# One PSUM bank per tile in a pair of half products, and branch weights loaded with a pair's first product

## The chip, the cores and the metric

The kernel runs on one core of one Trainium2 chip. The metric is the device time of one execution in microseconds (us). Times shown are medians of a few executions.

## What is computed

Two layers of a streaming encoder for 640 rows (512 of a prompt and 8 x 16 of decoding requests) of width 1024. Each layer projects its input once, with one wide matrix, splits the columns among four branches (a gated MLP, a recurrence, a latent attention, a memory attention) and their gates, and merges the branches:

```
(a_u, a_v, a_g, b_x, b_g, c_q, c_kv, c_kr, c_g, m_q, gate_logits) = split_cols(x @ w_in)
oa, ob, oc, om = the four branches, three of them times silu of a_g, b_g, c_g
g = sigmoid(gate_logits).reshape(B, T, N_BRANCH, D_MODEL)
ya, yb, yc, ym = oa @ w_br_a, ob @ w_br_b, oc @ w_br_c, om @ w_br_m
merged = g[:, :, 0] * ya + g[:, :, 1] * yb + g[:, :, 2] * yc + g[:, :, 3] * ym
x_new = layer_norm(ALPHA * x + merged @ w_out, ln_g, ln_b)
```

All data is float32. Every matrix operand is split into a high part, rounded to the format that TensorE multiplies, and a low part, the remainder; a product is high x high + high x low + low x high.

## The kernel before

**Pairs.** Most columns of `w_in` are done two chunks of 128 columns at a time, as a pair. A pair's product has two halves of output columns, two halves of the 1024 rows of contraction and two halves of the 640 time steps (`lo_` and `hi_`, 320 each). The kernel forms it by a scheme of seven half products in place of eight: sums of weight halves (`ws`, made by `wsum`) meet sums of input halves (`xt[1]` to `xt[4]`), and the results are added and subtracted on the way out. Each half product is one call of `product`: 12 matmuls of 128x128 weights by 320 columns, in one accumulation. `run_pair` writes the seven in this order: `ba` with input 11, `bb` with 21, `ba` with 2 (added to what is there), `bc` with 3, `ba` with 1, `bc` with 4, `ba` with 22. Between them, ScalarE copies a partial result of `ba` or `bc` to SBUF (`copy_out`, line 375) and VectorE adds or subtracts one (`psum`, line 372). Because `ba` and `bc` go on accumulating after such a copy, the next product into the same bank has to wait for it.

**PSUM.** There are eight banks, all given out: tag `acc` has two tiles of two banks each, tag `s` two tiles of one bank, tags `t` and `o` one bank each. `run_pair` takes one `acc` tile, named `fp`, and uses its two banks as `ba` and `bb`; `bc` is a tile of tag `s`, named `fp_c`. The framework puts a wait on an instruction by tile: an instruction that writes a tile waits for the engines that read that tile.

**Weights.** A pair's two raw chunks `r0`, `r1` and a branch's raw weights share the tag `raw`, three buffers, loaded on the queue of SyncE (SP), which works in order. A load waits until the last reader of its buffer is done. `wcast` (ScalarE, line 379) makes the high part, `wlow` (VectorE, line 384) the low part; high parts have three buffers, low parts two.

**Two kinds of pairs.** Each layer has six pairs without a branch (`gelu_pair`, `silu_pair`), whose results are stored, and 14 pairs in `merge_pairs`, whose results are gates: each of these is followed by two branch products `y` (`Branch.run`, `merge_y`, line 121), of 24 matmuls each for branches 0 to 2 and 12 for branch 3. VectorE multiplies a gate by its `y` (line 1112) and adds it to the sum `macc` (line 1116). The two `y` products also take tiles of tag `acc`, so a pair and its branch use three of them in turn.

**What sets the order.** `on` ties products, copies, casts and sums of the pairs on PE, ScalarE (ACT) and VectorE (DVE) to the order in which the code is written; the framework's scheduler places everything else (transposes, the recurrence, layer norms) between them, by its own estimates.

Of the kernel before, what the change touches and what calls it, by code (L numbers as in the profile page):

```python
# [21 lines left out]
TH = T // 2  # L22
# [17 lines left out]
def encoder_step(  # L40
# [30 lines left out]
    def tmp(shape, name="tmp", dtype=F32):  # L71
        return tp.tile(shape, dtype, tag="t", name=name)

    def ftmp(shape, name, dtype=F32):
        return tp.tile(shape, dtype, tag="f", name=name, bufs=2)
# [4 lines left out]
    def acc(name="acc"):  # L80
        return pa.tile([128, 2, 512], F32, tag="acc", name=name)

    def bank_s(name="ps_s"):
        return pb.tile([128, 512], F32, tag="s", name=name, bufs=2)
# [13 lines left out]
    def wtile(tag, n, name, bufs=2):  # L98
        return wp.tile([128, n], F32 if tag in ("raw", "ws") else F32R, tag=tag, name=name, bufs=bufs)

    def wraw(src, n=1024):
        raw = wtile("raw", n, "raw", 3)
        nc.sync.dma_start(out=raw, in_=src)
        return raw
# [95 lines left out]
    for l in range(L):  # L200
# [162 lines left out]
        def on(eng, ins_):  # L363
            order_only(ins_, tail.get(eng))
            tail[eng] = ins_
            return ins_

        def wsum(out, x, y):
            on("DVE", DVE.tensor_tensor(out=out, in0=x, in1=y, op=ALU.add))  # L369

        def psum(out, x, y, op):
            on("DVE", DVE.tensor_tensor(out=out, in0=x, in1=y, op=op))  # L372

        def copy_out(out, in_):
            on("ACT", ACT.copy(out=out, in_=in_))  # L375

        def wcast(src, n):
            h = wtile("wh", n, "wh", 3)
            on("ACT", ACT.copy(out=h, in_=src))  # L379
            return h  # L380

        def wlow(src, h, n):
            lo = wtile("wl", n, "wl")
            on("DVE", DVE.tensor_tensor(out=lo, in0=src, in1=h.bitcast(F32), op=ALU.subtract))  # L384
            return h, lo
# [3 lines left out]
        class Pair:  # L389
# [3 lines left out]
            def load(self):  # L393
                self.r0, self.r1 = (wraw(ins["w_fm"][l, self.c + e]) for e in range(2))
# [22 lines left out]
        def product(o, hl, half, x, first, last):  # L417
            bh, bl = xt[x]
            h, lo = hl
            steps = [(k, h, b) for k in range(4) for b in (bh, bl)] + [(k, lo, bh) for k in range(4)]  # L420
            for n, (k, a, b) in enumerate(steps):
                k0 = half * 512 + k * 128
                on("PE", PE.matmul(  # L423
                    out=o, lhsT=a[:, k0:k0 + 128], rhs=b[:, k, :],
                    start=(first and n == 0), stop=(n == len(steps) - 1), skip_group_check=True,
                ))
# [9 lines left out]
        def run_pair(p, nxt, act, y=None):  # L436

            r0, r1 = p.r0, p.r1
            ab, bc = acc("fp"), bank_s("fp_c")[:, 0:TH]
            ba, bb = (ab[:, j, 0:TH] for j in range(2))  # L440
            z0, z1, t_ = ftmp([128, T], "z0"), ftmp([128, T], "z1"), tmp([128, T], "tu")
            p1, u = t_[:, lo_], t_[:, hi_]
            product(ba, p.w0, 0, 11, True, False)
            copy_out(p1, ba)
            p.low1()
            h2 = wcast(r1, 1024)
            product(bb, p.w0, 1, 21, True, True)
            psum(z0[:, lo_], p1, bb, ALU.add)
            act(0, lo_, z0, z0[:, lo_])
            w2 = wlow(r1, h2, 1024)  # L450
            wsum(r0[:, b_], r0[:, b_], p.ws[:, a_])
            product(ba, p.w1, 0, 2, False, False)
            copy_out(u, ba)
            h3 = wcast(r0[:, b_], 512)
            product(bc, p.w1, 1, 3, True, False)
            copy_out(z1[:, hi_], bc)
            w3 = wlow(r0[:, b_], h3, 512)
            if nxt:
                nxt.load()
            if y:  # L460
                y.cast()
            elif nxt:
                nxt.cast0()
                nxt.sums(0)
            product(ba, w2, 0, 1, False, False)
            psum(z1[:, hi_], z1[:, hi_], ba, ALU.subtract)
            if not y and nxt:
                nxt.sums(1)
            product(bc, w2, 1, 4, False, True)
            psum(z1[:, lo_], bc, u, ALU.subtract)  # L470
            if y:
                y.low()
            if nxt:
                if y:
                    nxt.cast0()
                else:
                    nxt.low0()
            act(1, slice(0, T), z1, z1)
            if not y and nxt:
                nxt.cast1()  # L480
            product(ba, w3, 0, 22, False, True)
            act(0, hi_, z0, ba)
            if y:
                if nxt:
                    nxt.low0()
                    nxt.sums(0)
                    nxt.sums(1)
                    nxt.cast1()
                y.run((z0, z1))

        def gelu_pair(p, nxt):
            def act(e, cols, z, v_):
                on("ACT", ACT.activation(out=ub[:, p.c - FM_U + e, cols], in_=v_, func=AF.Gelu_apprx_tanh))

            run_pair(p, nxt, act)

        def silu_pair(p, nxt, i, c):
            th = [tmp([128, T], f"th{e}") for e in range(2)]
            rest = []

            def act(e, cols, z, v_):
                on("ACT", ACT.activation(out=th[e][:, cols], in_=v_, func=AF.Tanh, scale=0.5))
                rest.append((e, cols, v_))

            run_pair(p, nxt, act)
            for e, cols, v_ in sorted(rest, key=lambda r: -r[0]):
                on("DVE", DVE.scalar_tensor_tensor(
                    out=th[e][:, cols], in0=th[e][:, cols], scalar=1.0, in1=v_, op0=ALU.add, op1=ALU.mult
                ))
            for e in range(2):  # L510
                nc.gpsimd.dma_start(out=gscr[i][c + e], in_=th[e])
# [621 lines left out]
        class Branch:  # L1133
# [2 lines left out]
                self.br = (0, 2, 1, 3)[bi]  # L1136
                self.src = ins["w_brm"][l] if bi == 3 else ins["w_br"][l, self.br]

            def cast(self):
                self.raw = wtile("raw", 2 * self.n, "raw", 3)  # L1140
                nc.sync.dma_start(
                    out=self.raw.rearrange("p (e c) -> p e c", e=2),
                    in_=self.src[self.f:self.f + 2].rearrange("e p c -> p e c"),
                )
                self.h = wcast(self.raw, 2 * self.n)

            def low(self):
# [17 lines left out]
        def merge_pairs(bhl):  # L1165
            bhls[0] = bhl
            ys = [Branch(0, f) for f in (4, 6)] + [Branch(bi, f) for bi in (1, 2, 3) for f in (0, 2, 4, 6)]
            ps = [Pair(22 + y.br * 8 + y.f) for y in ys]
            first_pair(ps[0])
            for n, y in enumerate(ys):  # L1170
                def act(e, cols, z, v_):
                    on("ACT", ACT.activation(out=z[:, cols], in_=v_, func=AF.Tanh, scale=0.5))

                run_pair(ps[n], ps[n + 1] if n + 1 < len(ps) else None, act, y)
                if y.bi == 3 and y.f == 0:
                    merge_split(0)
            for f in (2, 4, 6):
                merge_split(f)
# [221 lines left out]
```

## Time and profile before

| | |
|---|---|
| median of 3 runs | 1487.37 us (1486.15 to 1489.79) |
| the profiled execution, its own time | 1489.98 us |
| span of the profile | 1488.2 us |
| TensorE matmul (PE) busy | 1390.5 us, 93% of the span |
| VectorE (DVE) busy | 985.9 us, 66% |
| ScalarE (ACT) busy | 637.8 us, 43% |
| GpSimd (POOL) busy | 124.3 us, 8% |
| DMA | 183.96 MB, 124 GB/s over the span |

Busy time of PE is from the start of a matmul to its end; matmuls overlap, so the time between two starts is shorter than one lasts. What is left of the span, some 98 us, is time in which no matmul runs at all.

### The profile page before, as it was taken

How to read it: one execution, taken by the hardware profiler on the slowest of the kernel's cores; microseconds unless marked ns; L12 is line 12 of the kernel's file. 1: busy time of each engine (PE TensorE's matmuls, PEld its weight loads, DVE VectorE, ACT ScalarE, POOL GpSimd, SP SyncE). 2: the span in 40 equal slices, each digit the busy share in tenths (PEclk: the TensorE clock that was granted, in tenths of full speed). 3: DMA queues.
4: the chain of work that ended last, by engine and by line, in shares of the span. 5: the costliest groups of instructions: out<-in, count | busy, mean ns of one | idle time of the engine just before them, and what ended most of it. 6: DMA issues, size and time to landing. Idle time of an engine off the chain costs nothing. (4 is left out here: it accounts for less than half of the span.)

```text
span 1488.2 us, 22595 instructions
## 1 busy us (share of the span) xinstructions
PE 1390.5 (93%) x8896; PEld 1257.4 (84%) x8896; DVE 985.9 (66%) x1676; ACT 637.8 (43%) x1159; POOL 124.3 (8%) x254
## 2 busy tenths in 40 slices
PE   8998999999899999999999989999998999899997
PEld 7788887779888988988888988877898889888886
DVE  8767747695656565666885776685855565667656
ACT  6543534455533333444255435444663333334430
POOL 1101100021200000000111012001111000000000
PEclk9999999999999999999999999999999999999999
DMA  7624623244232322236375246132443223222343
GB/s 272 256 79 167 189 77 118 82 172 141 94 98 89 99 71 79 78 93 205 107 229 183 96 152 220 33 118 97 163 143 113 77 78 103 82 76 67 95 146 106
DMA packets 59098, 183.96 MB, mean 124 GB/s; under 512 B 6640, under 2 KB 15760, under 8 KB 55920
## 3 DMA queue, kind: packets, MB, share of 16 engines
q1 hardware_dynamic: 48304, 127.54, 26.9%
q0 software_dynamic: 10688, 54.98, 10.0%
q8 instruction: 70, 1.15, 0.3%
q14 instruction: 36, 0.29, 0.1%
HBM read 148.49 MB, written 32.69 MB: 122 GB/s over the span
## 5 line engine op out<-in xcount | busy, mean ns | idle before, releaser
L384 DVE TENSOR_TENSOR wl<-raw,wh 128x1024 fp32r<-128x1024 f32 (+1 forms) x148 | 153.5, 1049 | 113.6 <-PE fp_c L423 56.7
L379 ACT CAST wh<-raw 128x1024 fp32r<-128x1024 f32 (+1 forms) x148 | 132.3, 910 | 108.8 <-DMA raw<-in_w_br 83.5
L423 PE MATMUL fp<-xh,wh 128*128 128x320 f32 x480 | 147.5, 319 | 24.9 <-ACT tu L375 22.4
L121 PE MATMUL y<-bhl,wh 128*128 128x320 f32 x896 | 145.9, 313 | 12.7 <-ACT wh L379 12.7
L121 PEld LDWEIGHTS y<-bhl,wh 128*128 128x128 f32 x896 | 134.1, 189 | 18.3 <-ACT wh L379 17.9
L423 PE MATMUL fp<-xl,wh 128*128 128x320 f32 x480 | 142.6, 309 | 0.0
L423 PE MATMUL fp<-xt,wh 128*128 128x320 f32 x640 | 110.9, 315 | 27.3 <-DVE z L372 27.3
L423 PEld LDWEIGHTS fp<-xt,wh 128*128 128x128 f32 x640 | 95.5, 188 | 37.4 <-DVE z L372 37.4
L423 PEld LDWEIGHTS fp<-xh,wh 128*128 128x128 f32 x480 | 90.0, 188 | 36.7 <-ACT tu L375 32.5
L121 PE MATMUL fm<-xl,wh 128*128 128x320 f32 x448 | 113.9, 327 | 0.0
L121 PE MATMUL fm<-xh,wh 128*128 128x320 f32 x448 | 112.6, 323 | 0.0
L423 PE MATMUL fp_c<-xt,wh 128*128 128x320 f32 x640 | 106.8, 309 | 0.0
L423 PEld LDWEIGHTS fp_c<-xt,wh 128*128 128x128 f32 x640 | 97.2, 188 | 0.0
L375 ACT COPY tu<-fp 128x320 f32<-128x320 f32 x80 | 34.0, 426 | 139.5 <-PE fp L423 138.5
L423 PEld LDWEIGHTS fp<-xl,wh 128*128 128x128 f32 x480 | 90.2, 188 | 0.1
L423 PE MATMUL fp<-xh,wl 128*128 128x320 f32 x480 | 89.9, 309 | 0.0
L147 DVE TENSOR_TENSOR wl<-raw,wh 128x1024 fp32r<-128x1024 f32 (+3 forms) x67 | 73.9, 1104 | 20.7 <-ACT wh L146 8.3
L146 ACT CAST wh<-raw 128x1024 fp32r<-128x1024 f32 (+3 forms) x67 | 63.9, 953 | 54.8 <-PE fm L121 17.7
L121 PE MATMUL fm<-xh,wl 128*128 128x320 f32 x448 | 86.3, 328 | 0.0
L121 PEld LDWEIGHTS fm<-xl,wh 128*128 128x128 f32 x448 | 75.7, 188 | 8.3 <-issue 6.4
L379 ACT CAST wh<-ws 128x1024 fp32r<-128x1024 f32 x40 | 41.8, 1046 | 91.7 <-DVE ws L369 91.7
L121 PEld LDWEIGHTS fm<-xh,wh 128*128 128x128 f32 x448 | 75.6, 188 | 6.1 <-issue 5.3
(340 smaller groups left out, 2816.5 us busy)
## 6 DMA issues: line engine op xcount, KB each, us to landing
raw<-in_w_fm SPq DMA_DIRECT2D x108, 512.0 KB, 3.7
xsum<-xt POOLq DMA_DIRECT2D x8, 1280.0 KB, 10.6
xt<-xsum POOLq DMA_DIRECT2D x8, 1280.0 KB, 6.1
raw<-in_w_br SPq DMA_DIRECT2D x20, 512.0 KB, 3.6
mcache<-in_mem_kv SPq DMA_DIRECT2D x8, 1024.0 KB, 6.8
raw<-in_w_out SPq DMA_DIRECT2D x16, 512.0 KB, 4.3
osrc<-oscr POOLq DMA_DIRECT2D x20, 320.0 KB, 3.1
gscr<-th POOLq DMA_DIRECT2D x16, 320.0 KB, 2.7
```

The lines of the kernel that those rows point to most:

```text
L121: PE.matmul(out=out[:, j, 0:TH], lhsT=a(k), rhs=b(k)[:, j * TH:(j + 1) * TH], start=(n == 0), stop=(n == len(steps) - 1),)
L146: ACT.copy(out=dst_h, in_=src)
L147: DVE.tensor_tensor(out=dst_l, in0=src, in1=dst_h.bitcast(F32), op=ALU.subtract)
L375: on("ACT", ACT.copy(out=out, in_=in_))
L379: on("ACT", ACT.copy(out=h, in_=src))
L384: on("DVE", DVE.tensor_tensor(out=lo, in0=src, in1=h.bitcast(F32), op=ALU.subtract))
L423: on("PE", PE.matmul(out=o, lhsT=a[:, k0:k0 + 128], rhs=b[:, k, :], start=(first and n == 0), stop=(n == len(steps) - 1), skip_group_check ...
```

## The change

In `run_pair`, `ba` becomes the first bank of an `acc` tile named `fp_a` (its second bank stays unused), and `bb` and `bc` become two tiles of tag `s`, `fp_b` and `fp_c`. In `Branch`, the load of the raw weights moves out of `cast` into a method of its own, `load`, which `run_pair` calls ahead of its first product; `cast` stays where it was, after the load of the next pair's weights.

```
@@ run_pair
             r0, r1 = p.r0, p.r1
-            ab, bc = acc("fp"), bank_s("fp_c")[:, 0:TH]
-            ba, bb = (ab[:, j, 0:TH] for j in range(2))
+            ba = acc("fp_a")[:, 0, 0:TH]
+            bb, bc = (bank_s(f"fp_{n}")[:, 0:TH] for n in "bc")
+            if y:
+                y.load()
             z0, z1, t_ = ftmp([128, T], "z0"), ftmp([128, T], "z1"), tmp([128, T], "tu")
             p1, u = t_[:, lo_], t_[:, hi_]
             product(ba, p.w0, 0, 11, True, False)
@@ class Branch
-            def cast(self):
+            def load(self):
                 self.raw = wtile("raw", 2 * self.n, "raw", 3)
                 nc.sync.dma_start(
                     out=self.raw.rearrange("p (e c) -> p e c", e=2),
                     in_=self.src[self.f:self.f + 2].rearrange("e p c -> p e c"),
                 )
+
+            def cast(self):
                 self.h = wcast(self.raw, 2 * self.n)
```

**TensorE, a pair of the first layer's merge.** The last matmuls of the first half product (into `ba`), the second (into `bb`) and the start of the third (into `ba` again), with the engines whose semaphores a row waits for in brackets. Before:

```order
L423 MATMUL fp<-xh_0_103,wl 128x320 x4
L423 MATMUL fp<-xh_1_104,wh 128x320 [waits Activation_49]
L423 MATMUL fp<-xl_1_106,wh 128x320
...
L423 MATMUL fp<-xh_1_104,wl 128x320 x4
L423 MATMUL fp<-xt_3984,wh 128x320 [waits DVE_49]
L423 MATMUL fp<-xt_3984,wh 128x320 x7
L423 MATMUL fp<-xt_3984,wl 128x320 x4
```

With the change:

```order
L423 MATMUL fp_a<-xh_0_103,wl 128x320 x4
L423 MATMUL fp_b<-xh_1_104,wh 128x320
L423 MATMUL fp_b<-xl_1_106,wh 128x320
...
L423 MATMUL fp_b<-xh_1_104,wl 128x320 x4
L423 MATMUL fp_a<-xt_3990,wh 128x320 [waits Activation_49]
L423 MATMUL fp_a<-xt_3990,wh 128x320 x7
L423 MATMUL fp_a<-xt_3990,wl 128x320 [waits DVE_49]
```

The second product no longer waits for ScalarE; the third waits for ScalarE (the copy of `ba`) where it waited for VectorE (the read of `bb`), and its last four matmuls name VectorE, which makes their low weights. All other pairs show the same.

**SyncE's queue, the start of the first layer's merge** (`in_w_fm` are the pairs' chunks, `in_w_br` a branch's weights, `vec` a small table). Before:

```order
L103 DMA raw<-in_w_fm 128x1024 x4
L519 DMA vec<-in_vecs 128x162
L1141 DMA raw<-in_w_br 128x2x512
L103 DMA raw<-in_w_fm 128x1024 x2
L1141 DMA raw<-in_w_br 128x2x512
```

With the change:

```order
L103 DMA raw<-in_w_fm 128x1024 x2
L1143 DMA raw<-in_w_br 128x2x512
L103 DMA raw<-in_w_fm 128x1024
L521 DMA vec<-in_vecs 128x162
L103 DMA raw<-in_w_fm 128x1024
L1143 DMA raw<-in_w_br 128x2x512
L103 DMA raw<-in_w_fm 128x1024 x2
```

A branch's load stood behind both chunks of the next pair; it now stands ahead of them.

**ScalarE, the first pair of the first layer's merge,** from the copy of the third product (`tu<-fp`) on; `lb` is the recurrence's work. Before:

```order
L1029 ACT_TABLE_LOAD
L1029 ACTIVATE lb_2996<-lb_2996 128x664
L1172 ACT_TABLE_LOAD
L1172 ACTIVATE z_4008<-z_4008 128x320
L375 COPY tu<-fp 128x320
L379 CAST wh<-raw 128x512
L375 COPY z_4009<-fp_c 128x320
L947 ACTIVATE ne<-ne 128x4
L379 CAST wh<-raw 128x1024 x2
```

With the change:

```order
L1176 ACTIVATE z_4017<-z_4017 128x320
L375 COPY tu<-fp_a 128x320
L1031 ACT_TABLE_LOAD
L1031 ACTIVATE lb_3002<-lb_3002 128x664
L379 CAST wh<-raw 128x512
L375 COPY z_4018<-fp_c 128x320
L379 CAST wh<-raw 128x1024 x2
L1176 ACT_TABLE_LOAD
L1176 ACTIVATE z_4018<-z_4018 128x640
```

A table load and the recurrence's square root moved from ahead of the copy of the third product to between it and the copy of the fourth (`z<-fp_c`). Elsewhere the scheduler moved a few transposes, `mix` matmuls and layer-norm steps between the pairs without a branch; the order of the pairs' own work is the same on every engine.

## Rows read from the trace of the kernel before

**Rows 1.** The page's first part: busy time, share of the span, instructions of each engine.

```profile
PE 1390.5 (93%) x8896; PEld 1257.4 (84%) x8896; DVE 985.9 (66%) x1676; ACT 637.8 (43%) x1159; POOL 124.3 (8%) x254
```

**Rows 2.** PE's waits, longest first: total us, times, longest.

```profile
PE fp L423 <- DVE z L372: 29.1, 42, 1.5
PE fp L423 <- ACT tu L375: 22.4, 36, 1.3
PE y L121 <- ACT wh L379: 12.7, 20, 2.3
```

**Rows 3.** PE's groups: busy, mean ns | idle before them, by releaser.

```profile
L423 PE MATMUL fp<-xh,wh 128*128 128x320 f32 x480 | 147.5, 319 | 24.9 <-ACT tu L375 22.4 <-DVE z L372 1.8 <-DVE mixb L660 0.4
...
L423 PE MATMUL fp<-xt,wh 128*128 128x320 f32 x640 | 110.9, 315 | 27.3 <-DVE z L372 27.3
```

**Rows 4.** PE's timeline over one merge pair: start, us, instruction [idle before <-releaser].

```profile
525.51 0.75 PE L423 MATMUL fp<-xh,wl 128*128 128x320 f32 x4
526.77 0.41 PE L423 MATMUL fp<-xh,wh 128*128 128x320 f32 x1 [0.52 <-ACT tu L375]
...
528.04 0.75 PE L423 MATMUL fp<-xh,wl 128*128 128x320 f32 x4
529.45 1.44 PE L423 MATMUL fp<-xt,wh 128*128 128x320 f32 x8 [0.65 <-DVE z L372]
...
531.31 1.34 PE L423 MATMUL fp_c<-xt,wh 128*128 128x320 f32 x8
...
533.07 1.34 PE L423 MATMUL fp<-xt,wh 128*128 128x320 f32 x8
...
537.76 0.75 PE L423 MATMUL fp<-xh,wl 128*128 128x320 f32 x4
539.67 2.61 PE L121 MATMUL y<-bhl,wh 128*128 128x320 f32 x16 [1.15 <-ACT wh L379]
...
549.24 0.41 PE L423 MATMUL fp<-xh,wh 128*128 128x320 f32 x1 [0.52 <-ACT tu L375]
```

**Rows 5.** ACT and DVE in the same pair, timeline of all engines.

```profile
526.29 0.43 ACT L375 COPY tu<-fp 128x320 f32<-128x320 f32 x1 [3.57 <-PE fp L423]
...
528.90 0.49 DVE L372 TENSOR_TENSOR z<-tu,fp 128x320 f32<-128x320 f32 x1 [1.67 <-PE fp L423]
...
538.57 2.00 ACT L379 CAST wh<-raw 128x1024 fp32r<-128x1024 f32 x2 [4.53 <-DMA raw<-in_w_br]
```

**Rows 6.** SyncE's loads in the same pair, timeline of the SP queue.

```profile
530.55 0.33 SPq L103 DMA_DIRECT2D raw<-in_w_fm  x1
534.62 0.38 SPq L1141 DMA_DIRECT2D raw<-in_w_br  x1
```

**Rows 7.** The page's DMA issues: count, size, median us to landing.

```profile
raw<-in_w_fm SPq DMA_DIRECT2D x108, 512.0 KB, 3.7
```

**Rows 8.** A later merge pair, of branch 3: its first product, and its third product's low weights.

```profile
647.40 0.31 PE L423 MATMUL fp<-xh,wh 128*128 128x320 f32 x1
...
650.18 1.22 DVE L384 TENSOR_TENSOR wl<-ws,wh 128x1024 fp32r<-128x1024 f32 x1
```

**Rows 9.** A pair without a branch: the last product waits behind a load.

```profile
142.18 0.33 SPq L103 DMA_DIRECT2D raw<-in_w_fm  x1
...
147.42 0.69 DVE L369 TENSOR_TENSOR ws<-raw 128x512 f32<-128x512 f32 x1 [1.75 <-DMA raw<-in_w_fm]
...
148.75 0.48 DVE L372 TENSOR_TENSOR z<-z,fp 128x320 f32<-128x320 f32 x1
...
149.29 0.41 PE L423 MATMUL fp<-xh,wh 128*128 128x320 f32 x1 [0.91 <-DVE z L372]
```

**Rows 10.** First merge pair of a layer: waits for ACT, in layers 1 and 2.

```profile
393.65 0.42 PE L423 MATMUL fp<-xh,wh 128*128 128x320 f32 x1 [1.32 <-ACT tu L375]
...
1147.20 3.63 PE L121 MATMUL y<-bhl,wh 128*128 128x320 f32 x16 [2.29 <-ACT wh L379]
```

**Rows 11.** A window after that wait: us, busy of each engine, granted clock, DMA share, GB/s.

```profile
1147.00:1152.00 5.00, 4.80 (x22) 4.80 (x23) 3.65 (x4) 2.06 (x4) 1.07 (x2) 0.66 0.66 220
```

More of the change, by code (lines that the diff above doesn't have):

```diff
@@ L438, in run_pair @@
             r0, r1 = p.r0, p.r1
-            ab, bc = acc("fp"), bank_s("fp_c")[:, 0:TH]
-            ba, bb = (ab[:, j, 0:TH] for j in range(2))
+            ba = acc("fp_a")[:, 0, 0:TH]
+            bb, bc = (bank_s(f"fp_{n}")[:, 0:TH] for n in "bc")
+            if y:
+                y.load()
             z0, z1, t_ = ftmp([128, T], "z0"), ftmp([128, T], "z1"), tmp([128, T], "tu")
@@ L1137, in __init__, with load @@
                 self.src = ins["w_brm"][l] if bi == 3 else ins["w_br"][l, self.br]
-            def cast(self):
+            def load(self):
                 self.raw = wtile("raw", 2 * self.n, "raw", 3)
@@ L1144, in cast @@
                 )
+            def cast(self):
                 self.h = wcast(self.raw, 2 * self.n)
```

## The prediction

> **What bounds the kernel now.** The page's first part comes first: PE is busy for 93% of the span, VectorE for 66% and ScalarE for 43% [rows 1]. So the time is PE's own work plus the 97.7 us in which it stands still (1488.2 - 1390.5), and a change that touches no matmul can only give back part of the second. Next I read PE's list of waits. Three of its lines make 64.2 us of the 97.7, and the change touches the code of all three: half products waiting for `z` on VectorE (29.1 us, 42 times), half products waiting for `tu` on ScalarE (22.4 us, 36 times), and branch products waiting for a high part on ScalarE (12.7 us, 20 times) [rows 2].
>
> Which products wait is told by their inputs. Inputs 1 to 4 bear the name `xt`, inputs 11, 21 and 22 the names `xh` and `xl`. PE's groups put 27.3 of the 29.1 us at a product that starts with `xt`, and only 1.8 us at one that starts with `xh` [rows 3]. In the timeline of one pair the picture is plain [rows 4]: the second product starts 0.52 us late, after the copy `tu`; the third starts 0.65 us late, after `z`; the branch product starts 1.15 us late. The second product writes `bb`, and the copy reads `ba`; the third writes `ba`, and `z` reads `bb` [rows 5]. They meet only because both banks are one tile.
>
> **What a wait costs.** A record of idle time is not the whole loss, since matmuls overlap. Two undisturbed products of 12 matmuls start 1.76 us apart (531.31 and 533.07), so a matmul takes 0.147 us of the engine, while its record lasts 0.31 us [rows 4]. A wait that the trace calls 0.52 us therefore also loses 0.31 - 0.147 = 0.163 us of overlap, and the first record after it is 0.10 us longer (0.41 for 0.31, 1.44 for 1.34). I add 0.265 us to each wait. The check: from the second product of this pair (526.77) to that of the next (549.24) are 22.47 us. The pair's seven products and the two of `y` are 84 + 48 = 132 matmuls, 19.36 us; the three waits with their additions are 0.785 + 0.915 + 1.415 = 3.115 us; together 22.48 us. Nothing else is lost in a pair.
>
> **The change, part by part.**
>
> Tiles of their own. The order of the changed kernel has no wait ahead of the second product, and ScalarE's copy in place of VectorE's `z` ahead of the third. The copy has been done since before the second product's start would have been (it ends 0.43 us after it begins at 526.29, and the second product alone lasts 1.76 us [rows 4, 5]), so its wait is covered. Hence all 36 waits for `tu` go: 22.4 + 36 x 0.265 = 31.9 us. Of the waits for `z`, those ahead of `xt` go; three of the 42 lie ahead of `xh` (the last product, after a read of `ba` itself), so 27.3 + 39 x 0.265 = 37.6 us.
>
> What is late next in a merge pair? The third product's low weights, which VectorE makes after the last `y` of the pair before. In the tightest pairs, those of branch 3 (84 + 24 matmuls), they are done at 650.18 + 1.22 = 651.40, which is 4.0 us after the pair's start at 647.40 [rows 8]; without waits PE needs them after 32 matmuls, 4.7 us. A margin of 0.7 us: covered, but not by much.
>
> Loads. A branch's load was issued at 534.62, as the next pair's second chunk was at 530.55, each when a buffer came free, and ScalarE then waited 4.53 us for it [rows 5, 6]. With the change it goes out a pair's length earlier, and its 20 waits go: 12.7 + 20 x 0.265 = 18.0 us. The queue holds as many loads as before; what moves back are the next pair's chunks, to the two times that I just named. The second of them would be issued at about 534.6 and land 3.7 us later (the median of 108 such loads [rows 7]), at 538.3; VectorE adds the chunks only after the low weights of `y` and of the next pair, which follow the last product (it ends near 538.5 [rows 4]) and take over a microsecond. Covered by about 1.5 us. If a load were later than that, the sums would be late, then VectorE's product with `y`, then the `acc` tile that the next pair wants.
>
> The long wait of a layer's first branch product (2.29 us) has a second price: behind it 16 matmuls take 3.63 us where 2.61 us is usual, and the granted clock of the 5 us from 1147 is 0.66, that is, part of it at 1.2 GHz in place of 2.4 [rows 4, 10, 11]. Without the wait 3.63 - 2.61 = 1.0 us more comes back.
>
> What stays. In a pair without a branch the last product (22) waits for a read of `ba` that stands on VectorE behind the sums of the next pair's chunks, and these behind a load, whose buffer comes free in the same pair: issued at 142.18, used at 147.42, then `z` at 148.75 and the product at 149.29, 0.91 us late [rows 9]. If the third product starts 0.92 us earlier, this chain starts only with the second product's end, and the last product may wait that much longer. Five such pairs per layer have a next pair, ten in all: from 0 (the load is early enough) to 10 x 0.915 = 9.2 us. I take 4 us, nearer the lower end, because only three waits of this sort are in the trace. In the first merge pair of each layer, ScalarE and VectorE carry the recurrence (waits of 1.32 us in place of 0.52 [rows 10]), and the new order puts a table load and a square root ahead of the copy that the fourth product of `bc` needs. Two waits of about 1 us may stay there per layer: 4 us, between 0 and the 10 us that stand there now (1.32, up to 1.5 ahead of the third product [rows 2], and 2.29, with additions, twice).
>
> A rule against the change is in the Trainium skill, page Perfetto Trace Analysis, section Matmul Optimizations: all eight PSUM banks should be in use, so that instructions overlap. The change leaves the second bank of `fp_a` idle and uses both one-bank tiles in every pair, with none to spare. By the rows, `bb` was read by 528.90 + 0.49 = 529.39 and is written again at 549.24 [rows 4, 5]; some 20 us lie between, so by them one tile for each is enough, and by the rule the waits would come back as those for a free bank.
>
> **The sum.** 31.9 + 37.6 + 18.0 + 1.0 - 4 - 4 = 80.5 us. The profiled execution took 1489.98 us (span 1488.2 us and 1.8 us around it), so 1409.5 us for such a one; it lies 2.6 us above the median of the runs (1487.37), which gives 1406.9. I predict 1407 us.
>
> **The rivals.**
>
> 1. *The waits are handed on.* PE comes 2 to 3 us earlier per pair, VectorE has the same work, and the third product waits for its low weights, or the last for `z`, in place of `bb`. For it: VectorE is at 66% over all, and the margin in branch 3's pairs is 0.7 us [rows 1, 8]. Against it: in 20 of the 28 merge pairs PE's work is 24 matmuls longer, 3.5 us more room. If the whole of the `z` term stays, 1407 + 37.6 = 1445 us; if it stays in the eight pairs of branch 3 and in all those without a branch, 8 x 0.915 + 9.2 - 4 = 12.5 us, so about 1420 us.
>
> 2. *Only the loads count.* The framework still orders the reads by something that the order does not show, and the products wait as before: 18.0 + 1.0 us come back, 1468 us. Against it is the order itself, which has no wait there.
>
> 3. *Banks run short* (what the Trainium skill's rule on the eight banks would bring). `fp_b` of the next pair would wait for a reader of the one before; at the price of today's wait for `z` in all 40 pairs that is again about 1445 us. The 20 us of room speak against it.
>
> 4. *Slower: the pairs' chunks come late.* The second chunk is now loaded when the branch's weights were, and a late one holds up VectorE's sums, the product with `y` and the next pair's `acc` tile. To eat the 80 us in the 28 merge pairs it would have to hold PE 2.9 us in each. With 1.5 us of cover and some 2 us of VectorE's work that could still slip, this begins at a landing of about 3.7 + 1.5 + 2 + 2.9 = 10 us; above that the kernel is slower. The median is 3.7 us, and ScalarE's wait of 4.53 us for the load issued at 534.62 ended with that load's landing, some 4 us after its issue [rows 5 to 7].
>
> **How the numbers follow.** The forecast, with its own range of 1397 to 1419 us (all 87.5 + 1 us back and a little at the layer's end, or both remainders at their upper ends and 4 us more), has a chance of 0.78. The smaller form of rival 1 (1419 to 1430) has 0.10, its whole form with rival 3 0.07, rival 2 0.02, rival 4 0.02, anything else 0.01. The range of 1396 to 1429 us holds a little over 8 in 10. What a measurement of this kernel can tell from no change is about 0.3%, 4.5 us. Only rival 4, and what I do not see, end within that or above it: faster 0.96, within 0.3% 0.02, slower 0.02.
>
> **What the profile of the changed kernel would show.** PE's waits for `tu` and for `z` ahead of `xt` are gone from its list, or below 3 us each; `y` for ScalarE below 2 us. A merge pair of branches 0 to 2 takes 19.4 us, one of branch 3 15.9 us. PE's busy time falls by the additions alone, 95 x 0.265 = 25 us, to about 1365 us, its idle time from 97.7 to some 43 us, and its share rises to 97%. ScalarE's waits for `in_w_br` are gone. What would prove me wrong: a new line in PE's waits of more than 10 us, for `wl` of line 384 or for a load; or VectorE waiting for `in_w_fm` in the merge.

## The result, and the profile after

The changed kernel takes 1407.31 us (median of four runs, 1406.80 to 1408.88) where the kernel before took 1486.76 us on the same chip (1485.60 to 1489.79). The ratio is 0.9464, with a 95% interval of 0.9448 to 0.9481: 5.4% faster, 79.4 us. 1407 us was predicted.

The first part of the page answers to [rows 1]: busy time, share of the span (now 1405.5 us), instructions.

```profile
PE 1367.4 (97%) x8896; PEld 1257.8 (89%) x8896; DVE 986.3 (70%) x1676; ACT 645.5 (46%) x1159; POOL 122.7 (9%) x254
```

The count of matmuls is the same. PE's busy time is 23.1 us lower and its idle time 38.1 us (1405.5 - 1367.4) in place of 97.7. VectorE and ScalarE do what they did before, in a shorter time.

PE's list of waits, against [rows 2] (total us, times, longest):

```profile
PE fp_a L423 <- DVE z L372: 7.9, 11, 2.4
...
PE y L121 <- ACT z L1176: 0.2, 1, 0.2
```

The line for `tu` is gone. What is left for `y` is a single wait of 0.2 us, and it is for another releaser (ScalarE's read of `fp_a`, line 1176, and not the cast `wh`). For `z`, 7.9 us stand where 29.1 stood. None of them is at an input named `xt`, as PE's groups tell, which answer to [rows 3]; in the timeline all eleven waits stand at product 22:

```profile
L423 PE MATMUL fp_a<-xt,wh 128*128 128x320 f32 x640 | 106.9, 309 | 0.0
L423 PE MATMUL fp_a<-xh,wh 128*128 128x320 f32 x320 | 98.1, 318 | 8.4 <-DVE z L372 7.9 <-DVE mixb L662 0.4
```

The timeline of one merge pair, all engines, answers to [rows 4 to 6] (start, us, instruction, idle before it):

```profile
522.28 0.31 PE L423 MATMUL fp_a<-xh,wh 128*128 128x320 f32 x1
523.22 1.22 DVE L384 TENSOR_TENSOR wl<-ws,wh 128x1024 fp32r<-128x1024 f32 x1
524.04 0.31 PE L423 MATMUL fp_b<-xh,wh 128*128 128x320 f32 x1
524.24 0.43 ACT L375 COPY tu<-fp_a 128x320 f32<-128x320 f32 x1 [4.32 <-PE fp_a L423]
525.80 1.34 PE L423 MATMUL fp_a<-xt,wh 128*128 128x320 f32 x8
526.07 0.49 DVE L372 TENSOR_TENSOR z<-tu,fp_b 128x320 f32<-128x320 f32 x1 [0.90 <-PE fp_b L423]
527.73 0.33 SPq L103 DMA_DIRECT2D raw<-in_w_fm  x1
530.32 0.33 SPq L103 DMA_DIRECT2D raw<-in_w_fm  x1
534.69 0.38 SPq L1143 DMA_DIRECT2D raw<-in_w_br  x1
536.00 0.68 DVE L369 TENSOR_TENSOR ws<-raw 128x512 f32<-128x512 f32 x1
541.64 0.31 PE L423 MATMUL fp_a<-xh,wh 128*128 128x320 f32 x1
```

Product follows product at 1.76 us (522.28, 524.04, 525.80), while the copy of `ba` runs beside the second and the read of `bb` beside the third. From pair to pair it is 19.36 us (541.64 - 522.28), where it was 22.47 in the pair of [rows 4] and 21.5 to 21.7 in most others of this length. The branch weights loaded at 534.69 are those of the pair that begins at 541.64. No releaser stands behind any row of PE.

### The profile page after: what moved, and what is told of

Same layout as the page of the kernel before. It is cut to its first block, busy times and chain, and to the rows that moved or that the text cites. A ratio compares the mean times of both kernels' runs of the same rounds, so it can differ in the third digit from the quotient of the medians.

```text
span 1405.5 us, 22592 instructions
## 1 busy us (share of the span) xinstructions
PE 1367.4 (97%) x8896; PEld 1257.8 (89%) x8896; DVE 986.3 (70%) x1676; ACT 645.5 (46%) x1159; POOL 122.7 (9%) x254
## 3 DMA queue, kind: packets, MB, share of 16 engines
q8 instruction: 70, 1.15, 0.3%
## 4 chain that ended last, share of the span: by engine, by line
PE 80%; DVE 10%; DMA 4%; issue 3%; ACT 2%; POOL 0%; DVEq 0%; SPq 0%; ACTq 0%
PE fp_a L423 17%; PE y L121 13%; PE fm L121 13%; PE y_ps L1249 8%; PE fp_c L423 7%; PE fp_b L423 5%; PE sc_ps L837 3%; PE v L136 2%; DMA raw<-in_w_fm 2%; PE c L136 2%; PE pv_ps L861 2%; PE pt_ps L854 1%; DVE wl L384 1%; PE q_ps L121 1%; DVE wl L147 1%
## 5 line engine op out<-in xcount | busy, mean ns | idle before, releaser
L121 PE MATMUL y<-bhl,wh 128*128 128x320 f32 x896 | 142.9, 310 | 0.2 <-ACT z L1176 0.2
L423 PE MATMUL fp_a<-xt,wh 128*128 128x320 f32 x640 | 106.9, 309 | 0.0
L423 PE MATMUL fp_a<-xh,wh 128*128 128x320 f32 x320 | 98.1, 318 | 8.4 <-DVE z L372 7.9
L423 PEld LDWEIGHTS fp_a<-xt,wh 128*128 128x128 f32 x640 | 97.2, 188 | 0.0
L423 PE MATMUL fp_a<-xl,wh 128*128 128x320 f32 x320 | 96.8, 314 | 0.0
L375 ACT COPY tu<-fp_a 128x320 f32<-128x320 f32 x80 | 34.0, 425 | 128.3 <-PE fp_a L423 126.7
L147 DVE TENSOR_TENSOR wl<-raw,wh 128x1024 fp32r<-128x1024 f32 (+3 forms) x67 | 74.0, 1105 | 21.7 <-ACT wh L146 8.5
L121 PE MATMUL y<-bhl,wl 128*128 128x320 f32 x448 | 76.1, 309 | 0.0
L121 PEld LDWEIGHTS fm<-xh,wl 128*128 128x128 f32 x448 | 67.9, 188 | 5.8 <-issue 5.1
L423 PEld LDWEIGHTS fp_a<-xh,wh 128*128 128x128 f32 x320 | 61.4, 192 | 11.8 <-DVE z L372 11.1
```

The lines of the kernel that those rows point to most:

```text
L121: PE.matmul(out=out[:, j, 0:TH], lhsT=a(k), rhs=b(k)[:, j * TH:(j + 1) * TH], start=(n == 0), stop=(n == len(steps) - 1),)
L147: DVE.tensor_tensor(out=dst_l, in0=src, in1=dst_h.bitcast(F32), op=ALU.subtract)
L423: on("PE", PE.matmul(out=o, lhsT=a[:, k0:k0 + 128], rhs=b[:, k, :], start=(first and n == 0), stop=(n == len(steps) - 1), skip_group_check ...
```

## The experiments

All are compared with the kernel before on the same chip, whose median was 1486.97, 1487.20 and 1486.64 us in the three sets (e1 to e4; e5, e6 and e9; e10). These medians and the 1486.76 us of the result lie within 0.6 us, which bounds what the chip can add where two of the versions are set against each other.

### One part at a time

**e1_banks_only** keeps the three PSUM tiles and puts the load back into `cast`.

```
             def cast(self):
+                self.load()
                 self.h = wcast(self.raw, 2 * self.n)
...
-            if y:
-                y.load()
```

> The three PSUM tiles as changed, the branch's load back behind the next pair's chunks. Theory (the terms add up): the branch waits return as they stood, 20 of them, 12.7 + 5.3 us, and perhaps the 1 us of the slow clock, so about 1426 us (1422 to 1430). Rival (PE, earlier by 1.7 us per pair, meets a load that is no earlier): each of the 20 waits grows by up to 1.7 us, about 1460 us.

Measured: 1420.88 us, ratio 0.9551 (0.9533 to 0.9569), a little below the expected range and far from the rival. The banks alone give 66.1 us, 5 more than on top of the load (1468.39 of e2 - 1407.31 = 61.1). PE's wait for the branch weights is left, but less of it than in [rows 2]:

```profile
PE y L121 <- ACT wh L379: 9.8, 21, 1.3
```

Most of these waits are as they were. The second pair of branch 2, a usual one, in e1 and under it in the kernel before, where its second product starts at 549.24 [rows 4]:

```profile
529.55 0.31 PE L423 MATMUL fp_b<-xh,wh 128*128 128x320 f32 x1
...
535.82 0.38 SPq L1141 DMA_DIRECT2D raw<-in_w_br  x1
...
540.51 2.61 PE L121 MATMUL y<-bhl,wh 128*128 128x320 f32 x16 [0.24 <-ACT wh L379]
```

```profile
556.53 0.38 SPq L1141 DMA_DIRECT2D raw<-in_w_br  x1
...
561.23 2.61 PE L121 MATMUL y<-bhl,wh 128*128 128x320 f32 x16 [0.25 <-ACT wh L379]
```

Counted from the second product's start, the load goes out after 6.27 us (535.82 - 529.55) where it took 7.29 (556.53 - 549.24), and PE comes to `y` after 10.72 us (540.51 - 0.24 - 529.55) where it took 11.74. Both are 1.02 us earlier, so the wait stays. What has shrunk are the waits in the first pair of a branch: these six were 8.8 us together and are 5.2 here, while the others went from 3.9 to 4.6. The first pair of branch 2 in e1, and under it VectorE in the same pair of the kernel before, whose other rows are in [rows 4 to 6]:

```profile
509.25 0.31 PE L423 MATMUL fp_b<-xh,wh 128*128 128x320 f32 x1
...
513.42 1.55 DVE L150 SCALAR_TENSOR_TENSOR bhl<-osrc,bhl 128x640 fp32r<-128x640 f32 x2
514.89 0.68 DVE L384 TENSOR_TENSOR wl<-raw,wh 128x512 fp32r<-128x512 f32 x1
515.61 0.38 SPq L1141 DMA_DIRECT2D raw<-in_w_br  x1
...
520.65 2.61 PE L121 MATMUL y<-bhl,wh 128*128 128x320 f32 x16 [0.68 <-ACT wh L379]
```

```profile
531.04 1.55 DVE L150 SCALAR_TENSOR_TENSOR bhl<-osrc,bhl 128x640 fp32r<-128x640 f32 x2
533.13 0.82 DVE L150 SCALAR_TENSOR_TENSOR bhl<-osrc,bhl 128x640 fp32r<-128x640 f32 x1 [0.53 <-ACT bhl L149]
533.87 0.69 DVE L384 TENSOR_TENSOR wl<-raw,wh 128x512 fp32r<-128x512 f32 x1
```

The load follows VectorE's last read of a buffer (`wl<-raw`, line 384). In such a pair VectorE also splits the new branch's inputs (`bhl`, line 150): three of these stood ahead of that read, here two. So the load goes out after 6.36 us (515.61 - 509.25) in place of 7.85 (534.62 - 526.77), 1.49 us sooner, with PE only 1.02 us sooner, and the wait is 0.68 us where it was 1.15. And the longest wait of all is 1.09 us in place of 2.29, and the window behind it (1105 to 1110) has a granted clock of 1.00 in place of 0.66 [rows 11]. The 2.9 us of waits and some 1.7 us of clock (0.34 of 5 us) make most of the 5 us. So the waits weren't quite independent: a part of the branch waits goes with the banks.

**e2_load_only** keeps the load ahead of the first product and puts the `fp` tile of two banks back.

```
-            ba = acc("fp_a")[:, 0, 0:TH]
-            bb, bc = (bank_s(f"fp_{n}")[:, 0:TH] for n in "bc")
+            ab, bc = acc("fp"), bank_s("fp_c")[:, 0:TH]
+            ba, bb = (ab[:, j, 0:TH] for j in range(2))
```

> The early branch load alone, with the two-bank tile as before. Theory: 18 to 19 us of the 1487 us come back, about 1468 us (1464 to 1472), and the waits for tu and z stay at 22 and 29 us. Rival (the pair's second chunk, now loaded later, holds up VectorE): more than 1475 us, with VectorE waiting for in_w_fm in the merge.

Measured: 1468.39 us, ratio 0.9873 (0.9859 to 0.9888). As foretold: 18.6 us back, the waits for `tu` (22.4 us, 36 times) and for `z` (29.2 us, 42 times) as in [rows 2], none for `y`. The load is worth 18.6 us to the kernel before and 13.6 us (1420.88 - 1407.31) once the banks are apart.

### One wait at a time

The next two are the changed kernel with one of the old waits put back by a dependency and nothing else: in **e3_copy_wait_back** the second product waits for the copy of `ba`, in **e4_z_wait_back** the third waits for the read of `bb`.

```
-            copy_out(p1, ba)
+            c1 = copy_out(p1, ba)
...
-            product(bb, p.w0, 1, 21, True, True)
+            product(bb, p.w0, 1, 21, True, True, c1)
```

> The changed kernel with one wait put back by hand: the second product's first matmul waits for ScalarE's copy of the first. Theory (a wait costs its idle time and 0.265 us of lost overlap): 40 waits of 0.52 us or a little more, about 32 us, so 1439 us (1435 to 1444). Rival (a wait costs its idle time alone): 22 us, 1429 us.

```
-            psum(z0[:, lo_], p1, bb, ALU.add)
+            d1 = psum(z0[:, lo_], p1, bb, ALU.add)
...
-            product(ba, p.w1, 0, 2, False, False)
+            product(ba, p.w1, 0, 2, False, False, d1)
```

> The changed kernel with the other wait put back: the third product's first matmul waits for VectorE's read of the second. Theory: 40 waits of 0.65 us and 0.265 us each, 37 us, of which some 4 us are given back because the last product of a pair without a branch then waits less; 1440 us (1436 to 1446), and e3 and e4 together add about 66 us. Rival (idle time alone): 26 us, 1433 us or less.

Measured: 1437.55 us for e3 (0.9671, 0.9655 to 0.9688) and 1437.59 us for e4 (0.9664, 0.9648 to 0.9680), so 30.2 and 30.3 us above the changed kernel. PE's waits, of e3 and then of e4:

```profile
PE fp_b L423 <- ACT tu L375: 23.0, 37, 1.3
PE fp_a L423 <- DVE z L372: 6.9, 8, 2.0
```

```profile
PE fp_a L423 <- DVE z L372: 31.1, 40, 2.2
```

In e3 the trace shows 22.0 us more idle time (23.0 less 1.0 at `z`) and 34 waits more, and the kernel loses 30.2: (30.2 - 22.0) / 34 = 0.24 us for each wait beside what is recorded as idle, against the 0.265 of the prediction. In e4 it is (30.3 - 23.2) / 29 = 0.24 as well. The second digit is not firm: the idle times are those of one traced execution each, and by that execution's own time it is 0.17 in e3 (1434.92 us) and 0.27 in e4 (1438.27 us), against the 1407.16 us of the changed kernel's, and neither figure counts the clock or the kernel's other waits, which differ from trace to trace. The idea that only the recorded idle time counts is out, since it gave 1429 us for e3 and at most 1433 for e4. PE's groups of e4 put 27.9 of the 31.1 us at `xt` and 3.2 at product 22, where the changed kernel has 7.9: when the third product starts late, product 22 waits less. This is the handing on for which the prediction kept 4 us.

The two waits together are worth 60.5 us (about 66 were expected); e2 against the changed kernel, which has both back at once, is 61.1. They add up.

### What is left of the waits for z

The timeline of a pair without a branch, changed kernel, answers to [rows 9]; under it windows around its last row and around the same product in the second layer (us, busy of each engine, granted clock, DMA share, GB/s):

```profile
137.41 0.33 SPq L103 DMA_DIRECT2D raw<-in_w_fm  x1
143.21 0.69 DVE L369 TENSOR_TENSOR ws<-raw 128x512 f32<-128x512 f32 x1 [3.24 <-DMA raw<-in_w_fm]
...
144.54 0.48 DVE L372 TENSOR_TENSOR z<-z,fp_a 128x320 f32<-128x320 f32 x1
...
145.08 0.41 PE L423 MATMUL fp_a<-xh,wh 128*128 128x320 f32 x1 [2.39 <-DVE z L372]
```

```profile
144.00:150.00 6.00, 4.92 (x23) 4.92 (x24) 5.80 (x9) 2.11 (x3) 1.49 (x3) 0.72 0.13 49
841.00:847.00 6.00, 5.58 (x27) 5.58 (x28) 5.26 (x8) 2.30 (x4) 1.08 (x2) 0.72 0.19 76
```

PE waits for VectorE by name, but VectorE sat 3.24 us with nothing to do, for a load, ahead of the read that PE wants. Nine of the eleven waits for `z` stand at product 22 of pairs without a branch (7.0 us). In both windows the granted clock is 0.72: for a part of each 1.2 in place of 2.4 GHz. **e5_sums_later** writes those sums behind the read.

```
             elif nxt:
                 nxt.cast0()
-                nxt.sums(0)
             product(ba, w2, 0, 1, False, False)
             psum(z1[:, hi_], z1[:, hi_], ba, ALU.subtract)
             if not y and nxt:
+                nxt.sums(0)
                 nxt.sums(1)
```

> In pairs without a branch the sums of the next pair's first chunk (line 369), which wait for that chunk's load, stand on VectorE ahead of the read of ba that product 22 waits for; here they stand behind it. Theory (what is left of the waits for z is this order on VectorE): the nine waits of product 22 in these pairs, 7.0 us, go with 9 x 0.265 = 2.4 us of lost overlap: about 9 us less, 1398 us, and PE's waits for z fall from 7.9 us to below 2. Rival (the wait is handed on): the sums come later by some 1.3 us, so do the low weights and sums of the next pair, and PE waits for wl or ws of lines 384 and 369 in place of z: 1407 us, no change.

Measured: 1399.47 us, ratio 0.9408 (0.9395 to 0.9420). PE's waits, and the window around the product of the first timeline:

```profile
PE fp_a L423 <- DVE wl L384: 2.6, 3, 1.1
...
PE fp_a L423 <- DVE z L372: 0.9, 2, 0.4
```

```profile
143.00:149.00 6.00, 5.15 (x35) 4.88 (x35) 5.91 (x9) 3.86 (x6) 1.08 (x2) 1.00 0.28 109
```

The waits for `z` are gone but for 0.9 us, and 2.6 us of the 7.0 come back as a wait for low weights: the theory is right and the rival holds for a third of it. A part of the gain is the clock: in the window it is 1.00 now, and so it is in the second layer (836 to 842). The two windows of 0.72 are worth some 1.7 us each (0.28 of 6 us); with 4.4 us of idle time (7.0 - 2.6) and six waits fewer at 0.24 us that makes 9.2, somewhat more than the 7.8 measured. This is the fastest version here, 7.8 us below the changed kernel.

### Banks

**e6_fp_b_in_o** gives `fp_b` of the merge pairs a bank that is idle there.

```
-            bb, bc = (bank_s(f"fp_{n}")[:, 0:TH] for n in "bc")
+            bb, bc = (b(f"fp_{n}")[:, 0:TH] for b, n in ((bank_o if y else bank_s, "b"), (bank_s, "c")))
```

> In the 28 merge pairs fp_b is a tile of tag o, which stands idle there, so fp_b and fp_c no longer take the two one-bank tiles of tag s in turn; all else is as in the changed kernel. Theory (one tile for each is enough, since some 20 us lie between the read of a bank and its next use): no change, 1407 us, within 2 us. Rival (banks run short): PE's remaining idle time in the merge pairs is waits for a free bank, and some of it goes; if half of the 38 us that PE still stands idle were that, 1388 us. The rival is what the Trainium skill, page Perfetto Trace Analysis, section Matmul Optimizations, would lead one to expect: all eight banks should be in use.

Measured: 1407.01 us, ratio 0.9459 (0.9446 to 0.9472): no change, and PE's wait for `z` is 7.9 us as in the changed kernel. No wait in the merge was one for the bank of `fp_b`.

### How much VectorE could still take

The prediction put the margin of the third product's low weights at 0.7 us in branch 3's pairs. **e9_vector_work** makes those weights three times, **e10_vector_half** (one copy of the added subtraction) twice.

```
             p.low1()
+            for _ in range(2 if y else 0):
+                on("DVE", DVE.tensor_tensor(
+                    out=p.w1[1], in0=p.ws, in1=p.w1[0].bitcast(F32), op=ALU.subtract
+                ))
```

> Each of the 28 merge pairs makes the low weights of its third product three times over in place of once: 2 x 1.22 = 2.44 us more on VectorE per pair (68 us in all), ahead of the third product; results are the same. Theory (VectorE's margin is 0.7 us in the pairs of branch 3, 84 + 24 matmuls, and some 3.5 us more in the others): only the eight pairs of branch 3 lose, about 2.44 - 0.7 + 0.265 = 2.0 us each, 16 us in all: 1423 us, with PE's new waits for line 384 in those pairs. Rival A (VectorE is busy for 70%, so 30% of 1400 us are free): no change, 1407 us. Rival B (VectorE runs level with PE in all merge pairs): all 68 us are lost, 1475 us.

Measured: 1438.04 us, ratio 0.9666 (0.9646 to 0.9687). That is 30.7 us lost: neither theory nor rivals. PE's waits, then both engines in a pair of branch 2 and PE in one of branch 3:

```profile
PE fp_a L423 <- DVE wl L449: 22.0, 23, 2.9
```

```profile
523.54 0.31 PE L423 MATMUL fp_a<-xh,wh 128*128 128x320 f32 x1
523.74 0.82 DVE L1118 SCALAR_TENSOR_TENSOR z<-z,y 128x640 f32<-128x640 f32 x1 [1.77 <-PE y L121]
524.48 1.22 DVE L384 TENSOR_TENSOR wl<-ws,wh 128x1024 fp32r<-128x1024 f32 x1
525.62 0.82 DVE L1122 TENSOR_TENSOR macc<-macc,z 128x640 f32<-128x640 f32 x1
526.35 2.48 DVE L449 TENSOR_TENSOR wl<-ws,wh 128x1024 fp32r<-128x1024 f32 x2
528.89 0.85 PE L423 MATMUL fp_a<-xt,wl 128*128 128x320 f32 x4 [0.49 <-DVE wl L449]
...
608.24 1.44 PE L423 MATMUL fp_a<-xt,wl 128*128 128x320 f32 x4 [2.94 <-DVE wl L449]
```

Six waits lie in pairs of branch 3 (2.94, 1.72 and 2.33 us, in both layers), near the size foretold (2.0 us a pair). The other seventeen, of mostly 0.49 us, lie where 3.5 us more room was expected: fifteen in pairs of branches 0 to 2, two in the first pair of branch 3 of each layer, which still follows a `y` of 24 matmuls. The waits make 22.0 + 23 x 0.265 = 28.1 of the 30.7 us; behind the longest of them the granted clock falls (last section), which can make the rest, though no run takes the two apart. The rows show why there is less room. VectorE stood idle for 1.77 us, but it reaches the low weights only behind its product with the last `y`, and that can't begin before the last `y` is done, which is when the new pair starts. The 24 matmuls more in such a pair lie ahead of that point and give no room behind it. The margin there is what lies between: low weights done 2.2 us after the pair's start in the changed kernel (523.22 + 1.22 - 522.28), needed at 4.7, so 2.5 us. The two subtractions (2.48 us) would just fit, but the addition into `macc`, behind the low weights in the changed kernel, runs ahead of them here and takes 0.73 us more (526.35 - 525.62). A revised theory from this was tried at half the load:

> As e9_vector_work, with one added subtraction of 1.22 us per merge pair in place of two (34 us in all). Revised theory (e9's trace: what counts is when VectorE comes to the third product's low weights after the last y, not how long a pair is): in the pairs of branches 0 to 2 the second subtraction would end 2.2 + 0.74 + 1.24 = 4.2 us after the pair's start, and PE needs it at 4.7, so nothing is lost there; in those of branch 3 e9's waits of 2.94, 1.72 and 2.33 us become some 1.7, 0.5 and 1.1, twice: 6.6 us and 6 x 0.265 = 1.6, so 8 us: 1415 us. Rival (the loss goes by the added work, whatever the pair): half of e9's 31 us, 1422 us.

Measured: 1412.09 us, ratio 0.9501 (0.9488 to 0.9514), so about 5 us lost. PE's waits:

```profile
PE fp_a L423 <- DVE wl L449: 5.2, 6, 1.7
```

Six waits, all in pairs of branch 3 and none elsewhere: the revised theory holds for the place. The loss is 3 us below its figure. In each layer the waits are 1.68, 0.46 and 0.46 us where 1.7, 0.5 and 1.1 were expected, which is 1.3 us of the 3; the rest stays open. The rival (1422) is out.

## Why the prediction was right, and where its terms were off

**The two bank waits: right.** All 36 waits for `tu` and all waits for `z` ahead of `xt` are gone. Both terms (31.9 and 37.6 us), less the remainders of 8 us, make 61.5; e2 against the changed kernel measures 61.1. The price of a wait beside its idle time came out at about 0.24 us (0.17 to 0.27) where 0.265 was taken. PE's busy time fell to 1367.4 us (about 1365 foretold), its idle time to 38.1 (43).

**The branch loads: right, but not independent of the banks.** 18.0 + 1.0 us were predicted, and 18.6 are what the load brings to the kernel before (e2). With the 61.1 us of the banks on top of it, that is the order in which the prediction added, and its terms come out. In the other order the banks bring 66.1 us and the load 13.6 (e1): both together bring 5 us less than the two measured alone (66.1 + 18.6 = 84.7), because a part of the branch waits shrinks with the banks. The expectation of e1 had missed that. The pair in which the prediction read this wait (1.15 us) is the first of a branch; 14 of the 20 waits are of 0.2 to 0.4 us.

**The remainders: near in sum, wrong in place.** The last product of pairs without a branch was given 4 us. The trace after has 7.0 us there, nine waits. The prediction counted three of them in the kernel before; by its timeline they are two (0.69 us at 85.17, 0.91 at 149.29), and the third (0.20 at 404.66) stands in a merge pair. That makes 5.4 us and 7 x 0.265 = 7.3 us more, and a wait of 1.2 us at `fp_c` in one such pair. The first merge pairs were given 4 us; the trace has two waits of 0.45 and 0.46 us there. e5 shows that the first remainder is due to the order on VectorE: without it 7.8 us come back, some of them by the clock.

**The clock: given back in two places, lost in two.** The slow stretch behind the long wait of `y` is gone: behind the same product, now at 1096.6, the window of 5 us has a granted clock of 1.00 (0.66 in [rows 11]). The kernel before had a second one, behind a wait of 2.01 us in the memory attention (`mso_ps`), which the prediction didn't see: 0.72 from 1031 to 1037. In the trace after this wait is 1.39 us, and the window from 987 to 993 has 1.00. But behind the two longest of the remaining waits for `z` (2.39 us at 145.08 and 1.92 us at 841.42) the clock falls to 0.72, in the windows above. Each of the four is worth some 1.7 us, so in sum the clock gave nothing back where 1.0 us was counted.

**The chunks' loads: safe, with a little more room.** The prediction said that the next pair's chunks would go out when the second chunk and the branch weights did, the second 7.85 us behind the start of the second product (534.62 - 526.77; 7.29 in a usual pair, by the rows of e1). In the usual pair of the changed kernel they go out at 527.73 and 530.32, the second 6.28 us behind that start (530.32 - 524.04); a load of this kind lands after 3.6 us (the page's median), and the sums start at 536.00. That leaves 2.1 us of cover, near the 1.5 that was foretold, and rival 4 never came near.

**The margin in branch 3's pairs: misread, and still covered.** The prediction read it in the third pair of that branch and called that the tightest. The tightest is the second, here in the changed kernel and under it in the kernel before:

```profile
596.20 0.31 PE L423 MATMUL fp_a<-xh,wh 128*128 128x320 f32 x1
...
599.59 1.22 DVE L384 TENSOR_TENSOR wl<-ws,wh 128x1024 fp32r<-128x1024 f32 x1
...
600.90 0.82 PE L423 MATMUL fp_a<-xt,wl 128*128 128x320 f32 x4
```

```profile
629.18 0.31 PE L423 MATMUL fp<-xh,wh 128*128 128x320 f32 x1
...
632.57 1.22 DVE L384 TENSOR_TENSOR wl<-ws,wh 128x1024 fp32r<-128x1024 f32 x1
```

The low weights are done at 600.81, 4.61 us after the pair's start, and PE needs them at 4.7: its row is 0.07 us longer than the usual 0.75, and that is all. In the kernel before they are done 4.61 us after the start too (632.57 + 1.22 - 629.18). So the change used up nothing on VectorE's side; without PE's waits the margin was 0.1 us there from the first, and not 0.7, and that it held is luck. In this pair VectorE also splits the first merged sums (`mg`, line 150) ahead of the low weights. Rival 1 did not come, but it was closer than its chance of 0.10 looks: e10 shows that 1.22 us of added work on VectorE per pair begin to cost there. The argument that pairs of branches 0 to 2 have 3.5 us more room was wrong (e9); they have 2.5 us in all, and had them before (low weights done at 526.49 in the pair that starts at 524.34, 2.15 us). The pairs of branch 3 start 15.8 to 15.9 us apart (15.9 foretold).

**Rivals 2 and 3 are out**, the one by the trace after and e1, where the banks give 66.1 us without the load, the other by the result and e6. The rule of the Trainium skill that rival 3 was priced from (Perfetto Trace Analysis, section Matmul Optimizations: use all eight banks) is not borne out here: a kernel that leaves half of a tile idle takes 1407 us and not the 1445 priced from the rule, and another bank for `fp_b` changes nothing. What counted was which half products share a tile.

**The sum.** 80.5 us were foretold and 79.4 measured. That it came so close is luck in part: the term for `tu` was 31.9 us and e3 gives 30.2, the first remainder was 4 us and the trace has some 8, the second 4 and about 1, and the clock gave nothing back in place of 1.0. PE's waits elsewhere in the kernel, which no term counts, fell from 24.7 us to 18.7 (2.4 of that at `y_ps`, after the merge; the other traces lie between 18.4 and 23.8). These errors offset each other.

## What to carry to other kernels

When an engine waits for the reader of a buffer that it is not about to write, look for two uses that share one tile: the wait goes with the tile, and cost here the recorded idle time and some 0.2 to 0.3 us more of lost overlap each time. Before adding up what several changes bring, ask whether one of them shortens the waits that another removes; here the two parts measured alone made 84.7 us, and together 79.4. Before calling a pair the tightest, go through all of them; the one read had 0.7 us of margin, the tightest 0.1. The margin of an engine is counted from the event that its next piece of work waits for, not from its share of busy time or the length of a stage: VectorE is busy for 70% here, and 2.44 us more per pair cost 31 us, half of that 5.

## What the runs showed of the hardware

Standing still is followed by a lower clock in some places and not in others. In e9, PE stood for 2.94 us ahead of 608.24, and the window of the 6 us about it has a granted clock of 0.55, so most of what it covers was at 1.2 GHz; PE's next four matmuls take 1.44 us, where behind a wait of 0.49 us they take 0.85 (the rows of e9 above). The windows of e9:

```profile
607.00:613.00 6.00, 4.76 (x18) 4.76 (x19) 3.34 (x5) 1.60 (x4) 0.00 (x0) 0.55 0.29 89
858.00:864.00 6.00, 5.98 (x41) 5.98 (x42) 5.12 (x8) 3.38 (x5) 1.08 (x2) 1.00 0.28 108
```

The second row is around this product 22:

```profile
858.02 0.42 PE L423 MATMUL fp_a<-xh,wh 128*128 128x320 f32 x1 [2.56 <-DVE z L372]
```

This wait of 2.56 us stands in the pair where the changed kernel's wait of 1.92 us (841.42) was followed by 0.72: here the window shows 1.00. So a long wait can cost more than its idle time and the lost overlap, and its length alone does not tell which one will; what does was not settled by these runs.
